# An encoder layer on one core: loads of the output projection issued two tiles ahead, stores moved to ScalarE's queue, and the down-projection's weight factors handed out in other places

## The chip, the cores and the metric

The kernel runs on one core of one Trainium2 chip. The metric is the device time of one execution in microseconds (us); below, times before are three runs and one profiled execution. The engines are TensorE (PE, with its weight loads as PEld), VectorE (DVE), ScalarE (ACT), GpSimd (POOL) and SyncE (SP), which here only issues DMAs. ACT and POOL can issue DMAs too; each engine works through its own list of instructions in order, and a DMA that waits holds up what is behind it on the engine that issues it.

## The reference

One layer of a hybrid encoder, for 2048 tokens of width 1024 and 16 meta tokens in front, all in float32:

```python
xn = rms_norm(h, g_pre_mix)
proj = xn @ w_in                       # q latent | kv latent | rotary key | S5 input
attn = mla_bidirectional(...)          # 8 heads, 512 columns
ssm  = S5 forward + backward, GELU, GLU   # 512 columns
mix = concat([rms_norm(attn, g1), rms_norm(ssm, g2)])
h = h + rms_norm(mix @ w_out, g_post_mix)
m = rms_norm(h, g_pre_mlp) @ w_mlp_up            # 1024 x 4096
m = square(relu(m)) @ w_mlp_down                 # 4096 x 1024
h = h + rms_norm(m, g_post_mlp)                  # meta tokens are dropped
```

## The kernel before, in words

Every float32 product is made of three matmuls: each operand is split (`split`, L125 to L127) into a rounded half, `h = copy(x)` on ACT (L126), and the rest, `l = x - h` on DVE (L127), and PE adds `h.h + h.l + l.h`. So each tile that goes into a product costs one ACT cast and one DVE subtraction; names end in `h` and `l` accordingly (`ah`, `al`, `wh`, `wl`).

The stages follow one another, with their edges overlapping: projections (to about 280 us of the span), attention with the S5 in its background (to about 1583), the output projection (to about 1850), the up-projection (to about 2508) and the down-projection (to the end). The function that emits a stage writes instructions in some order, but the kernel is built with `TileContext(nc, schedule_with_timeline_sim=True)`: a scheduler simulates the program and puts each engine's instructions in an order of its own, by the times at which they become ready there. So the order of the code sets which buffers there are and which loads exist, and the scheduler decides what stands where in each engine's list.

**Output projection.** There are 16 tiles of 128 tokens (`NT`). `out_tile(t)` (L1191) makes tile `t`, and prepares the attention half of tile `t+1` (`a_ops`, L1120) and the S5 half of tile `t+2` (`s_ops`, L1114). `s_ops` loads `sr` (128x4x128) from the DRAM buffer `SD`; `a_ops` loads `ar` from `AD` (attention's outputs, not divided by the sum yet) and, in two DMAs, `rb` from `RD2` (the reciprocals of the sums, broadcast over 64 rows each) and multiplies them on DVE (L1129). `halves` (L1104) splits the result, squares it on ACT (L1110) and sums it on DVE (`sq`, `aq`, L1111), for the norms of the two halves. `sr` and `rb` have one buffer each (`bufs=1`), `ar` two. PE makes `op` (L1183); ACT scales the attention half (`ot`, L1212) and DVE adds the S5 half (`o`, L1213). Then come the post norm (a square with a sum on ACT, `jk`, L1217; the root on POOL, L132 and L133; a product on DVE, L1219), the residual `xt`, whose load is emitted at the start of the tile (L1197) into one buffer, the store of `o` to `HD` (L1221, SP), and the pre norm of the MLP (`jk`, L1226; `hn`, L1228). `hn_T` (L1231) transposes `hn` on PE, ACT copies it to `hb`, and SP stores that to `HTD` in two DMAs (L1245). The first two tiles' S5 products are made ahead (`W["ps", t]`).

Attention's last work runs beside the first tiles: `X` (L612 to L614) adds up values from `ph` and `pl` (`pl = s - ph`, DVE L628); `o` is stored to `AD` and its sums to `RD` (L644, L645, SP), the sums come back as `rr` (L648, issued on POOL), DVE takes the reciprocal (L649) and POOL's queue writes `RD2` (L650).

**Up-projection.** 32 pairs, each with 84 matmuls for 256 hidden columns of 1024 tokens, in a scheme of seven products for 2x2 blocks (`pA`, `pB`, `pE`, `pF` are PSUM banks). `relu2` (L1352) takes a block through relu and square on ACT, makes sums on DVE and POOL (L1367 to L1373), and stores seven blocks of 256 KB per pair to `MD` (`put`, L1359, on SP). SP also loads 1 MB of weights (`raw`, L1254) and of transposed activations (`traw`, L1275).

**Down-projection.** 8 chunks `b` of 512 hidden columns, each with 4 groups `g` of 84 matmuls, again seven products (`pX`, `pY`, `pE`, `pF`, L1644) that are added to `acc`. `w_factors(b)` (L1531) is a generator: it loads the chunk's weights in two DMAs of 1 MB (`raw`) and yields 14 times, once for each weight factor (seven products times two halves `fp`). Four of the seven factors are sums of blocks: POOL makes them (`wst`, L1555), 14 instructions per chunk, then ACT and DVE split them. `m_factors` (L1565) loads `mraw` from `MD` and splits it. The loop over the groups passes `step` to `down`, which calls it after each product; there the generators are advanced:

```python
if g == 2 and i > 2:
    next(nwf, None)
elif g == 3:
    next(nwf, None)
    next(nwf, None)
```

Of the kernel before, what the change touches and what calls it, by code (L numbers as in the profile page):

```python
# [51 lines left out]
def hymba_layer_kernel(  # L52
# [1041 lines left out]
    def out_open():  # L1094
        ip = W["ip"] = ph.enter_context(pool("iO", 2, "right"))
        W["ep"] = ph.enter_context(pool("eO", 2, "right"))
        e1 = W["e1"] = ph.enter_context(pool("e1", 1, "right"))
        gpo = W["gpo"] = mk(e1, [128, D], "gpo")
        Y.dma_start(out=gpo, in_=g_post_mix[0].partition_broadcast(128))
        for t in range(2):  # L1100
            W["s", t] = s_ops(t)
            yield

    def halves(src, nm):  # L1104
# [6 lines left out]
        V.reduce_sum(out=sq, in_=src.rearrange("p k c -> p c k"), axis=AX.X)  # L1111
        return h, l, sq

    def s_ops(t):  # L1114
        cs = slice(t * 128, (t + 1) * 128)
        sr = W["ip"].tile([128, 4, 128], F32, tag="sr", name="sr", bufs=1)
        Y.dma_start(out=sr, in_=SD[:, cs].rearrange("(k p) c -> p k c", p=128))
        return halves(sr, "s")

    def a_ops(t):  # L1120
        cs = slice(t * 128, (t + 1) * 128)
        ar = W["ip"].tile([128, 4, 128], F32, tag="ar", name="ar")
        Y.dma_start(out=ar, in_=AD[:, cs].rearrange("(k p) c -> p k c", p=128))
        rb = W["ip"].tile([128, 4, 128], F32, tag="rb", name="rb", bufs=1)
        for b in range(2):
            src = RD2[b:b + 1, cs]
            Y.dma_start(out=rb[64 * b:64 * b + 64],
                        in_=bass.AP(src.tensor, src.offset, [[0, 64], [2 * 2048, 4], [1, 128]]))
        V.tensor_tensor(out=ar, in0=ar, in1=rb, op=ALU.mult)  # L1129
        return halves(ar, "a")  # L1130

# [57 lines left out]
        return sq, [out_mm(h, l, 4, half) for half in range(2)]  # L1189

    def out_tile(t, between):  # L1191
        if t + 1 < NT:
            W["a", t + 1] = a_ops(t + 1)
        if t + 2 < NT:
            W["s", t + 2] = s_ops(t + 2)
        xt = W["e1"].tile([128, D], F32, tag="xt", name="xt")
        Y.dma_start(out=xt, in_=xv[t // 8, t % 8])  # L1197
        sqs, ps = W.pop(("ps", t), None) or out_s(t)
        h, l, sqa = W.pop(("a", t))
        p = pa("ss")  # L1200
        T.matmul(out=p[:, 0:2], lhsT=sqa, rhs=ones)
        T.matmul(out=p[:, 2:4], lhsT=sqs, rhs=ones)
        s2 = sm.tile([128, 4], F32, tag="s2c", name="s2c")
        S.copy(out=s2, in_=p[:, 0:4])
        ra = rstd_of(s2[:, 0:1], 512)
        rb = rstd_of(s2[:, 2:3], 512, eps=4 * EPS)
        o = W["ep"].tile([128, D], F32, tag="o", name="o")
        for half in range(2):
            hs = slice(half * 512, (half + 1) * 512)
            p = out_mm(h, l, 0, half)  # L1210
            tm = W["e1"].tile([128, 512], F32, tag="ot", name="ot")
            S.activation(out=tm, in_=p, func=AF.Copy, scale=ra)  # L1212
            V.scalar_tensor_tensor(out=o[:, hs], in0=ps[half], scalar=rb, in1=tm, op0=ALU.mult, op1=ALU.add)  # L1213
        between()
        jk = W["e1"].tile([128, 512], F32, tag="ot", name="jk").bitcast(BF16)
        ss = sm.tile([128, 1], F32, tag="ss", name="ss")
        S.activation(out=jk, in_=o, func=AF.Square, accum_out=ss)  # L1217
        r = rstd_of(ss, D)
        V.scalar_tensor_tensor(out=o, in0=o, scalar=r, in1=W["gpo"], op0=ALU.mult, op1=ALU.mult)  # L1219
        V.tensor_tensor(out=o, in0=o, in1=xt, op=ALU.add)  # L1220
        Y.dma_start(out=HD[t], in_=o)  # L1221

        hn = wraw.tile([128, 8, 256], F32, tag="raw", name="raw")[:, 0:4].rearrange("p k c -> p (k c)") if t == NT - 1 else \
            W["e1"].tile([128, D], F32, tag="hn", name="hn", bufs=2)
        ss = sm.tile([128, 1], F32, tag="ss", name="ss")
        S.activation(out=jk, in_=o, func=AF.Square, accum_out=ss)  # L1226
        r = rstd_of(ss, D)
        V.scalar_tensor_tensor(out=hn, in0=o, scalar=r, in1=gpr, op0=ALU.mult, op1=ALU.mult)  # L1228
        return hn

    def hn_T(t, hn):  # L1231

        ct, i = t // 8, t % 8
        cs = slice((i % 4) * 128, (i % 4) * 128 + 128)
        ps = []
        for a in range(2):
            p = pa("hT")
            for k in range(4):
                T.transpose(out=p[:, k * 128:(k + 1) * 128], in_=hn[:, (4 * a + k) * 128:(4 * a + k + 1) * 128],
                            identity=ident)  # L1240
            ps.append(p)
        b = hn if t == NT - 1 else mk(tq, [128, D], "hb")
        for a in range(2):
            S.copy(out=b[:, a * 512:(a + 1) * 512], in_=ps[a])
            Y.dma_start(out=HTD[ct].rearrange("k p b c -> p k b c")[:, :, 2 * a + i // 4, cs],  # L1245
                        in_=b[:, a * 512:(a + 1) * 512].rearrange("p (k c) -> p k c", k=4))

    NP = FF // 256
# [24 lines left out]
    def s_load(ct, k):  # L1273
        RAW[ct, k] = raw = tst.tile([128, 4, 512], F32, tag="traw", name="traw")
        Y.dma_start(out=raw, in_=HTD[ct, k])  # L1275

    W["a", 0] = a_ops(0)
    for t in range(2):
        W["ps", t] = out_s(t)
# [72 lines left out]
    def relu2(c, src, n, odd, half):  # L1352

        S.activation(out=c, in_=src, func=AF.Relu)
        S.activation(out=c, in_=c, func=AF.Square)
        md = MD[n // NP, n % NP]

        def put(i, x):
            Y.dma_start(out=md[:, i], in_=x)  # L1359

        if (odd, half) != (0, 1):
            put({(0, 0): 0, (1, 0): 1, (1, 1): 5}[odd, half], c)
        blocks[odd, half] = c
        if len(blocks) == 4:
            a11, a12, a21, a22 = (blocks.pop(x) for x in ((0, 0), (1, 0), (0, 1), (1, 1)))
            s1, s2, s4 = rt(), rt(), rt()
            V.tensor_tensor(out=s1, in0=a21, in1=a22, op=ALU.add)  # L1367
            put(3, s1)
            V.tensor_tensor(out=a21, in0=a11, in1=a21, op=ALU.subtract)
            put(4, a21)  # L1370
            G.tensor_tensor(out=s2, in0=s1, in1=a11, op=ALU.subtract)
            put(2, s2)
            G.tensor_tensor(out=s4, in0=a12, in1=s2, op=ALU.subtract)  # L1373
            put(6, s4)
# [156 lines left out]
    def w_factors(b):  # L1531
# [9 lines left out]
        for first, *more in ((b11,), (b21,), (b22, (sub, b12), (add, b11)), (b12, (sub, b11)), (b22, (sub, b12)),  # L1541
                             (b22, (sub, b12), (add, b11), (sub, b21)), (b22,)):
            both = []
            for fp in range(2):
                def blk(x):
                    return raws[fp][:, x[0], x[1]]
# [5 lines left out]
                if more:  # L1552
                    st = wst.tile([128, 512], F32, tag="st", name="wst")
                    for op, x in more:
                        G.tensor_tensor(out=st, in0=src, in1=blk(x), op=op)  # L1555
                        src = st
                split(src, h, l)
                both.append((h, l))
# [134 lines left out]
    for n, (b, g) in enumerate(parts):  # L1693
# [4 lines left out]
        def step(i, behind):  # L1698
            if behind:
                next(nm, None)  # L1700
                if g == 2 and i > 2:
                    next(nwf, None)
                elif g == 3:
                    next(nwf, None)
                    next(nwf, None)
            elif n == 0:
                while len(WF) <= i:
# [1 line left out]

        down(b, g, step)  # L1710
        if g == 3:
            for _ in nwf:
                pass
            del WF[:7]


# [28 lines left out]
```

## Time and profile before

| | before |
|---|---|
| median of three runs | 3232.68 us (3231.8, 3232.68, 3236.42) |
| profiled execution | 3229.18 us |
| its span | 3227.4 us, so 1.8 us lie around it |
| mean granted TensorE clock | 0.964 |
| DMA | 329.93 MB, mean 102 GB/s |
| `MD` stores, `mraw` loads | 224 each, 256 KB |
| `HD` stores, `HTD` stores | 16 of 512 KB, 32 |
| weight loads of the down-projection | 16 of 1024 KB |

The profile shows one execution. In its tables an instruction stands as line, engine, operation, then output `<-` inputs; a wait is put down to the instruction or DMA that came last, in the form `[idle before <-releaser]`. "SPq" rows are DMAs that SP issued, with the time that issuing took, waits included. The table of windows gives, for each stretch of the span, the busy time of each engine with its count of instructions. The chain of waits goes back from the last instruction to what released it. Lines of all these are shown in the prediction where they are used.

### The profile page before, as it was taken

What the parts mean: (1) busy time and instruction counts of PE and PEld (TensorE: products, weight loads), DVE (VectorE), ACT (ScalarE), POOL (GpSimd) and SP (SyncE); (2) the same over time, 40 slices, a digit from 0 to 9 for tenths busy, and PEclk for the clock granted to TensorE, in tenths of its full rate; (3) what the DMA queues carried; (4) which work ended last, traced back from release to release, by engine and by line L of the source; (5) the groups of instructions that cost most, each with busy time, mean ns of one, the idle gap of its engine ahead of it and who ended that gap; (6) DMA issues with size and microseconds to landing.
All of it is one profiled execution on the core that took longest, in us unless ns stands there. A gap on an engine that the chain in (4) does not pass through costs nothing. (4 is left out here: it accounts for less than half of the span.)

```text
span 3227.4 us, 43434 instructions
## 1 busy us (share of the span) xinstructions
PE 2976.6 (92%) x14095; PEld 2361.9 (73%) x14095; DVE 2246.5 (70%) x3243; ACT 1763.7 (55%) x3345; POOL 1751.5 (54%) x2659
## 2 busy tenths in 40 slices
PE   6999988989999999999889789998999899999996
PEld 5899956656777766688667668887888677777774
DVE  6333278767888876675356587668767688888888
ACT  4333356988777799964445444545544433333343
POOL 4122245875888877600022287767767445555566
PEclk8999989999999999999999899999999999999998
DMA  4232231211000023231346445444544433333336
GB/s 151 62 86 74 69 78 27 60 43 33 24 15 26 26 70 90 67 117 49 70 146 191 148 129 174 154 152 149 173 150 151 133 114 111 117 112 111 111 121 202
DMA packets 300453, 329.93 MB, mean 102 GB/s; under 512 B 38736, under 2 KB 240848, under 8 KB 299200
## 3 DMA queue, kind: packets, MB, share of 16 engines
q1 hardware_dynamic: 298176, 325.44, 33.4%
q8 instruction: 111, 1.82, 0.2%
q10 hardware_dynamic: 1792, 1.57, 0.2%
q14 instruction: 118, 0.97, 0.1%
q0 software_dynamic: 256, 0.14, 0.0%
HBM read 206.47 MB, written 120.52 MB: 101 GB/s over the span
## 5 line engine op out<-in xcount | busy, mean ns | idle before, releaser
L628 DVE TENSOR_TENSOR pl<-s,ph 128x512 fp32r<-128x512 f32 x512 | 349.9, 685 | 164.8 <-ACT s L627 161.7
L624 ACT ACTIVATE ph<-s 128x512 fp32r<-128x512 f32 (+1 forms) x544 | 323.3, 595 | 168.7 <-PE s L622 155.5
L575 DVE TENSOR_REDUCE mx<-mxp 128x1 f32<-128x512 f32 x512 | 342.4, 683 | 55.7 <-PE mxp L574 52.6
L627 ACT ACTIVATE s<-s 128x512 f32<-128x512 f32 x512 | 304.1, 594 | 0.7
L126 ACT CAST ah<-mraw 128x512 fp32r<-128x512 f32 x224 | 138.8, 620 | 302.4 <-DMA mraw<-MD 216.0
L127 DVE TENSOR_TENSOR al<-mraw,ah 128x512 fp32r<-128x512 f32 x224 | 214.8, 964 | 73.5 <-ACT ah L126 68.2
L1266 POOL TENSOR_TENSOR st<-raw 128x512 f32<-128x512 f32 x120 | 179.9, 1501 | 135.2 <-DVE al L127 128.5
L620 PE MATMUL s<-ql,kh 96*128 96x512 f32 (+1 forms) x544 | 225.2, 414 | 14.7 <-ACT ZS L938 4.9
L612 PE MATMUL X<-pl,vt 128*65 128x512 f32 x512 | 209.4, 409 | 30.0 <-DVE pl L628 29.5
L621 PE MATMUL s<-qh,kl 96*128 96x512 f32 (+1 forms) x544 | 217.2, 399 | 0.0
L622 PE MATMUL s<-qh,kh 97*128 97x512 f32 (+1 forms) x544 | 214.5, 400 | 0.7 <-DMA qh<-nm 0.7
L574 PE MATMUL mxp<-kh,qh 96*128 96x512 f32 x512 | 199.0, 410 | 13.2 <-DVE mx L575 5.5
L132 POOL TENSOR_SCALAR rs_v<-ss 128x1 f32<-128x1 f32 (+1 forms) x98 | 21.8, 223 | 347.2 <-ACT kvn L325 119.1
L1666 POOL TENSOR_TENSOR acc<-acc,x 128x512 f32<-128x512 f32 x64 | 101.5, 1588 | 200.2 <-ACT x L1665 200.2
L613 PE MATMUL X<-ph,vt 128*64 128x512 f32 x512 | 204.8, 400 | 0.0
L1644 PE MATMUL pX<-wh,ah 128*128 128x512 f32 x384 | 160.2, 418 | 48.4 <-DVE acc L1653 48.1
L614 PE MATMUL X<-ph,vt 128*65 128x512 f32 x512 | 204.2, 399 | 0.0
L127 DVE TENSOR_TENSOR al<-st,ah 128x512 fp32r<-128x512 f32 x120 | 128.3, 1070 | 58.0 <-ACT ah L126 57.5
L1644 PE MATMUL pX<-wl,ah 128*128 128x512 f32 x384 | 156.7, 408 | 0.5 <-DVE wl L127 0.4
L126 ACT CAST ah<-st 128x512 fp32r<-128x512 f32 x120 | 74.1, 618 | 150.9 <-POOL st L1266 70.8
L1644 PE MATMUL pX<-wh,al 128*128 128x512 f32 x384 | 156.2, 407 | 0.0
L620 PEld LDWEIGHTS s<-ql,kh 96*128 96x128 f32 (+1 forms) x544 | 102.8, 189 | 62.2 <-DVE mx L575 7.5
(967 smaller groups left out, 9569.6 us busy)
## 6 DMA issues: line engine op xcount, KB each, us to landing
MD<-r SPq DMA_DIRECT2D x224, 256.0 KB
mraw<-MD SPq DMA_DIRECT2D x224, 256.0 KB
raw<-in_w_mlp_up_dram SPq DMA_DIRECT2D x32, 1024.0 KB
xt<-in_x_dram SPq DMA_DIRECT2D x32, 512.0 KB
raw<-in_w_mlp_down_dram SPq DMA_DIRECT2D x16, 1024.0 KB
ug<-UD SPq DMA_DIRECT2D x32, 256.0 KB
HD<-o SPq DMA_DIRECT2D x16, 512.0 KB
traw<-HTD SPq DMA_DIRECT2D x8, 1024.0 KB
```

The source lines that it names most:

```text
L126: S.copy(out=h, in_=src)
L127: eng.tensor_tensor(out=l, in0=src, in1=f(h), op=ALU.subtract)
L575: V.reduce_max(out=mxs[n][:, j, b:b + 1], in_=p, axis=AX.X)
L612: T.matmul(out=X[:65], lhsT=v[:, t, 0:65], rhs=pl_, start=(t == 0), stop=False)
L613: T.matmul(out=X[:64], lhsT=v[:, t, 65:129], rhs=ph_, start=False, stop=False)
L620: T.matmul(out=s[:m], lhsT=kh[0:96, cs], rhs=ql, start=True, stop=False)
L621: T.matmul(out=s[:m], lhsT=kl[:, cs], rhs=qh[0:96], start=False, stop=False)
L622: T.matmul(out=s[:m], lhsT=kh[:, cs], rhs=qh, start=False, stop=True)
L624: S.activation(out=ph_[:m], in_=s[:m], func=AF.Exp, scale=SCALE)
L627: S.activation(out=s, in_=s, func=AF.Exp, scale=SCALE)
L628: V.tensor_tensor(out=pl_, in0=s, in1=f(ph_), op=ALU.subtract)
L1644: T.matmul(out=ps, lhsT=x[:, c], rhs=y, start=(first and fp == 0 and j == 0), stop=(fp == 1 and j == 2), skip_group_check=not first)
```

## The change

Three parts.

1. Output projection. A new function `loads(t)` issues all of a tile's loads (`sr`, `xt`, `ar`, `rb`), and `out_tile(t)` calls it for `t+1` and `t+2` before it does anything else; `s_ops` and `a_ops` keep the arithmetic alone. `sr`, `rb` and `xt` have two buffers each now. The S5 half is prepared one tile ahead instead of two.
2. Stores. `HD`, `HTD` and three of the seven `MD` stores of a pair are issued by ACT (`S.dma_start`) and not by SP (`Y.dma_start`).
3. Down-projection. The generator of weight factors is advanced once per step, from the third step of group 2 over group 3 to the fourth of the next chunk's group 0, and not drained at the chunk's end. For chunk 0, the sums of `fp == 0` are made on DVE (V), not on POOL (G).

```diff
+    def sd_load(t):
+        cs = slice(t * 128, (t + 1) * 128)
+        W["sr", t] = sr = W["ip"].tile([128, 4, 128], F32, tag="sr", name="sr")
+        Y.dma_start(out=sr, in_=SD[:, cs].rearrange("(k p) c -> p k c", p=128))
+
     def s_ops(t):
-        cs = slice(t * 128, (t + 1) * 128)
-        sr = W["ip"].tile([128, 4, 128], F32, tag="sr", name="sr", bufs=1)
-        Y.dma_start(out=sr, in_=SD[:, cs].rearrange("(k p) c -> p k c", p=128))
-        return halves(sr, "s")
-
-    def a_ops(t):
+        return halves(W.pop(("sr", t)), "s")
+
+    def loads(t):
+
+        if ("x", t) in W:
+            return
+        if ("sr", t) not in W and t > 1:
+            sd_load(t)
+        W["x", t] = xt = tq.tile([128, D], F32, tag="xt", name="xt", bufs=2)
+        Y.dma_start(out=xt, in_=xv[t // 8, t % 8])
         cs = slice(t * 128, (t + 1) * 128)
         ar = W["ip"].tile([128, 4, 128], F32, tag="ar", name="ar")
         Y.dma_start(out=ar, in_=AD[:, cs].rearrange("(k p) c -> p k c", p=128))
-        rb = W["ip"].tile([128, 4, 128], F32, tag="rb", name="rb", bufs=1)
+        rb = W["ip"].tile([128, 4, 128], F32, tag="rb", name="rb")
+        W["ar", t] = ar, rb
         for b in range(2):
...
+    def a_ops(t):
+        ar, rb = W.pop(("ar", t))
         V.tensor_tensor(out=ar, in0=ar, in1=rb, op=ALU.mult)
...
     def out_tile(t, between):
+        for u in range(t + 1, t + 3):
+            if u < NT:
+                loads(u)
         if t + 1 < NT:
             W["a", t + 1] = a_ops(t + 1)
-        if t + 2 < NT:
-            W["s", t + 2] = s_ops(t + 2)
-        xt = W["e1"].tile([128, D], F32, tag="xt", name="xt")
-        Y.dma_start(out=xt, in_=xv[t // 8, t % 8])
+            if ("ps", t + 1) not in W:
+                W["s", t + 1] = s_ops(t + 1)
+        xt = W.pop(("x", t))
...
-        Y.dma_start(out=HD[t], in_=o)
...
         S.activation(out=jk, in_=o, func=AF.Square, accum_out=ss)
+        S.dma_start(out=HD[t], in_=o)
...
-            Y.dma_start(out=HTD[ct].rearrange("k p b c -> p k b c")[:, :, 2 * a + i // 4, cs],
+            S.dma_start(out=HTD[ct].rearrange("k p b c -> p k b c")[:, :, 2 * a + i // 4, cs],
...
-        def put(i, x):
-            Y.dma_start(out=md[:, i], in_=x)
+        def put(i, x, q=Y):
+            q.dma_start(out=md[:, i], in_=x)
 
         if (odd, half) != (0, 1):
-            put({(0, 0): 0, (1, 0): 1, (1, 1): 5}[odd, half], c)
+            put({(0, 0): 0, (1, 0): 1, (1, 1): 5}[odd, half], c, S)
...
-                        G.tensor_tensor(out=st, in0=src, in1=blk(x), op=op)
+                        (V if b == 0 and fp == 0 else G).tensor_tensor(out=st, in0=src, in1=blk(x), op=op)
...
-                if g == 2 and i > 2:
-                    next(nwf, None)
-                elif g == 3:
-                    next(nwf, None)
+                if (g == 2 and i > 2) or (g == 3 and i > 0) or (g == 0 and n > 0 and i < 4):
                     next(nwf, None)
...
         if g == 3:
-            for _ in nwf:
-                pass
             del WF[:7]
```

Since a scheduler decides the order, the places that matter are shown as the lists have them. First VectorE's list at the end of attention, from the first product `ar<-ar,rb` on (`pl` and `ph` are attention's, `ar`, `rb`, `al`, `aq` the attention half and `sr`, `sl`, `sq` the S5 half of an output tile; the numbers tell buffers apart). Before:

```order
L1129 TENSOR_TENSOR ar_19065<-ar_19065,rb_19067 128x512
L628 TENSOR_TENSOR pl_18954<-s_18948,ph_18952 128x512
L1111 TENSOR_REDUCE sq_18921<-sr_18915 128x128
L628 TENSOR_TENSOR pl_18966<-s_18960,ph_18964 128x512
L127 TENSOR_TENSOR al_19072<-ar_19065,ah_19071 128x512
L628 TENSOR_TENSOR pl_18978<-s_18972,ph_18976 128x512
L1111 TENSOR_REDUCE aq_19075<-ar_19065 128x128
L1129 TENSOR_TENSOR ar_19130<-ar_19130,rb_19132 128x512
L628 TENSOR_TENSOR pl_18990<-s_18984,ph_18988 128x512
L127 TENSOR_TENSOR sl_18939<-sr_18936,sh_18938 128x512
L127 TENSOR_TENSOR al_19137<-ar_19130,ah_19136 128x512
L628 TENSOR_TENSOR pl_19002<-s_18996,ph_19000 128x512
```

Now, from the same product on:

```order
L1143 TENSOR_TENSOR ar_19067<-ar_19067,rb_19069 128x512
L628 TENSOR_TENSOR pl_18954<-s_18948,ph_18952 128x512
L1112 TENSOR_REDUCE sq_18921<-sr_18915 128x128
L628 TENSOR_TENSOR pl_18966<-s_18960,ph_18964 128x512
L1112 TENSOR_REDUCE sq_18942<-sr_18936 128x128
L127 TENSOR_TENSOR al_19074<-ar_19067,ah_19073 128x512
L1143 TENSOR_TENSOR ar_19134<-ar_19134,rb_19136 128x512
L628 TENSOR_TENSOR pl_18978<-s_18972,ph_18976 128x512
L628 TENSOR_TENSOR pl_18990<-s_18984,ph_18988 128x512
L1112 TENSOR_REDUCE aq_19077<-ar_19067 128x128
L127 TENSOR_TENSOR al_19150<-ar_19134,ah_19149 128x512
L628 TENSOR_TENSOR pl_19002<-s_18996,ph_19000 128x512
```

The first product still stands ahead of the same `pl`. The second product stands one `pl` earlier, and no longer behind `aq` of the first. The next rows of the new list are `aq_19153` and then the third product; before, the third product came next, and the second's `aq` behind it. The line numbers of the new file are some 14 higher here.

Second, SyncE's list of DMAs, from the load of `rb` for the second product to the store of `RD`. Before:

```order
L1127 DMA rb_19132<-RD2_78 64x4x128 x2
L1117 DMA sr_18936<-SD_76 128x4x128
L1123 DMA ar_19218<-AD_75 128x4x128
L1127 DMA rb_19220<-RD2_78 64x4x128 x2
L1127 DMA rb_19308<-RD2_78 64x4x128
L1117 DMA sr_19143<-SD_76 128x4x128
L1127 DMA rb_19308<-RD2_78 64x4x128
L1123 DMA ar_19306<-AD_75 128x4x128
L1127 DMA rb_19437<-RD2_78 64x4x128 x2
L644 DMA AD_75<-o_19038 64x512
L645 DMA RD_77<-o_19038 1x512
```

Now:

```order
L1138 DMA rb_19136<-RD2_78 64x4x128 x2
L1138 DMA rb_19145<-RD2_78 64x4x128 x2
L1118 DMA sr_19139<-SD_76 128x4x128
L1118 DMA sr_19220<-SD_76 128x4x128
L1138 DMA rb_19226<-RD2_78 64x4x128 x2
L1133 DMA ar_19143<-AD_75 128x4x128
L1133 DMA ar_19224<-AD_75 128x4x128
L1138 DMA rb_19314<-RD2_78 64x4x128 x2
L1138 DMA rb_19443<-RD2_78 64x4x128 x2
L644 DMA AD_75<-o_19038 64x512
L645 DMA RD_77<-o_19038 1x512
```

What was one `rb` after the other, each behind a product, is now issued with two buffers ahead of the loads of `sr` and `ar`; the stores of `AD` and `RD`, which attention's end goes through, still stand behind the `rb` of two further tiles. The stores of `HD` and `HTD` further down are no longer in this list; they stand on ScalarE's, `HD` behind the second `jk`, `HTD` behind the copies to `hb`.

Third, GpSimd's list at chunk 0 of the down-projection, from the last sum of the up-projection (`r`) on; `wst` are the factor sums, `raw_26528` and `raw_26530` the weights of `fp` 0 and 1 of chunk 0, `raw_27160` and `raw_27162` those of chunk 1, `acc` the results. Before:

```order
L1373 TENSOR_TENSOR r_26658<-r_26629,r_26657 128x512
L1555 TENSOR_TENSOR wst_26788<-raw_26528 128x512
L1555 TENSOR_TENSOR wst_26794<-raw_26530 128x512
L1555 TENSOR_TENSOR wst_26822<-raw_26528 128x512
L1555 TENSOR_TENSOR wst_26828<-raw_26530 128x512
L1555 TENSOR_TENSOR wst_26858<-raw_26528 128x512
L1555 TENSOR_TENSOR wst_26858<-wst_26858,raw_26528 128x512
L1555 TENSOR_TENSOR wst_26866<-raw_26530 128x512
L1555 TENSOR_TENSOR wst_26858<-wst_26858,raw_26528 128x512
L1555 TENSOR_TENSOR wst_26866<-wst_26866,raw_26530 128x512
L1666 TENSOR_TENSOR acc_26685<-acc_26685,x3_26838 128x512
L1666 TENSOR_TENSOR acc_26685<-acc_26685,x3_26847 128x512
```

Now:

```order
L1390 TENSOR_TENSOR r_26658<-r_26629,r_26657 128x512
L1572 TENSOR_TENSOR wst_26794<-raw_26530 128x512
L1572 TENSOR_TENSOR wst_26828<-raw_26530 128x512
L1572 TENSOR_TENSOR wst_26866<-raw_26530 128x512
L1572 TENSOR_TENSOR wst_26866<-wst_26866,raw_26530 128x512 x2
L1683 TENSOR_TENSOR acc_26685<-acc_26685,x3_26838 128x512
L1683 TENSOR_TENSOR acc_26685<-acc_26685,x3_26847 128x512
L1572 TENSOR_TENSOR wst_27292<-raw_27160 128x512
```

The sums of `raw_26528` are gone from this list and stand on VectorE's, and the first sums of chunk 1 have moved ahead of the next `acc`. From the end of chunk 0 on, each engine's list of the changed kernel holds the same instructions in the same order as before.

More of the change, by code (lines that the diff above doesn't have):

```diff
@@ L1112, in halves @@
         return h, l, sq
+    def sd_load(t):
+        cs = slice(t * 128, (t + 1) * 128)
+        W["sr", t] = sr = W["ip"].tile([128, 4, 128], F32, tag="sr", name="sr")
+        Y.dma_start(out=sr, in_=SD[:, cs].rearrange("(k p) c -> p k c", p=128))
     def s_ops(t):
-        cs = slice(t * 128, (t + 1) * 128)
-        sr = W["ip"].tile([128, 4, 128], F32, tag="sr", name="sr", bufs=1)
-        Y.dma_start(out=sr, in_=SD[:, cs].rearrange("(k p) c -> p k c", p=128))
-        return halves(sr, "s")
-    def a_ops(t):
+        return halves(W.pop(("sr", t)), "s")
[3 more added lines that the diff above has]
+        if ("sr", t) not in W and t > 1:
+            sd_load(t)
+        W["x", t] = xt = tq.tile([128, D], F32, tag="xt", name="xt", bufs=2)
+        Y.dma_start(out=xt, in_=xv[t // 8, t % 8])
         cs = slice(t * 128, (t + 1) * 128)
@@ L1275, in s_load @@
         Y.dma_start(out=raw, in_=HTD[ct, k])
+    loads(0)
     W["a", 0] = a_ops(0)
```

## The prediction, made before the changed kernel had run

> **What bounds the kernel now.** The page first: TensorE (PE) is busy for 92% of the span.
>
> ```profile
> span 3227.4 us, 43434 instructions
> PE 2976.6 (92%) x14095; PEld 2361.9 (73%) x14095; DVE 2246.5 (70%) x3243; ACT 1763.7 (55%) x3345; POOL 1751.5 (54%) x2659
> ```
>
> The other 8%, 251 us, is what a change of order can win. The table of windows (length, then busy time of PE, PEld, DVE, ACT, POOL, then PE's clock, DMA share, GB/s) says where it lies; the rows are the end of attention, the output projection, the up-projection, chunk 0 of the down-projection with the start of chunk 1, and most of chunks 1 to 7.
>
> ```profile
> 1560.00:1640.00 80.00, 64.66 (x302) 50.12 (x301) 29.17 (x44) 27.37 (x53) 4.51 (x10) 0.91 0.39 92
> 1640.00:1860.00 220.00, 185.69 (x847) 148.39 (x846) 135.67 (x146) 105.94 (x201) 64.33 (x128) 0.94 0.58 166
> 1860.00:2500.00 640.00, 615.71 (x2663) 505.46 (x2664) 480.89 (x509) 315.95 (x553) 463.25 (x301) 0.98 0.47 154
> 2500.00:2640.00 140.00, 122.96 (x500) 97.57 (x499) 99.61 (x123) 62.69 (x112) 63.11 (x42) 0.93 0.41 127
> 2640.00:3150.00 510.00, 476.48 (x2036) 388.29 (x2035) 423.50 (x543) 177.27 (x315) 280.82 (x192) 0.97 0.38 114
> ```
>
> PE idles 15 us around attention's end, 34 in the output projection, 24 in the up-projection, 17 around chunk 0 and 34 in the chunks behind it. PE's timeline gives the pieces at attention's end (start, duration, instruction, idle before and its releaser):
>
> ```profile
> 1587.97 0.69 PE L612 MATMUL X<-pl,vt 128*65 128x512 f32 x1 [4.10 <-DVE pl L628]
> 1588.46 0.63 PE L613 MATMUL X<-ph,vt 128*64 128x512 f32 x1
> ...
> 1597.49 0.44 PE L612 MATMUL X<-pl,vt 128*65 128x512 f32 x1 [1.51 <-DVE pl L628]
> 1597.78 0.39 PE L613 MATMUL X<-ph,vt 128*64 128x512 f32 x1
> ...
> 1608.54 0.69 PE L612 MATMUL X<-pl,vt 128*65 128x512 f32 x1 [5.84 <-DVE pl L628]
> ...
> 1627.35 0.50 PE L1183 MATMUL op<-woh,ah 128*128 128x512 f32 x1 [2.60 <-ACT ot L1212]
> ...
> 1631.66 0.50 PE L1183 MATMUL op<-woh,sh 128*128 128x512 f32 x1 [1.28 <-DVE o L1213]
> ```
>
> The second matmul behind the gap of 4.10 us takes 0.63 us, the second behind that of 1.51 us 0.39. About ten matmuls go that slowly, 0.24 us more each, so a long gap costs some 2 us more than it shows. [...]
>
> VectorE (DVE) was late with `pl` because it stood at a product of the output projection that waits for a load:
>
> ```profile
> 1586.62 0.69 DVE L1129 TENSOR_TENSOR ar<-ar,rb 128x512 f32<-128x512 f32 x1 [7.59 <-DMA rb<-RD]
> ...
> 1596.14 0.69 DVE L1129 TENSOR_TENSOR ar<-ar,rb 128x512 f32<-128x512 f32 x1 [4.32 <-DMA rb<-RD]
> ...
> 1605.35 0.69 DVE L1129 TENSOR_TENSOR ar<-ar,rb 128x512 f32<-128x512 f32 x1 [5.44 <-DMA rb<-RD]
> ...
> 1615.62 0.69 DVE L1129 TENSOR_TENSOR ar<-ar,rb 128x512 f32<-128x512 f32 x1 [6.41 <-DMA ar<-AD]
> ...
> 1629.93 0.35 DVE L649 RECIPROCAL rr<-rr 128x32 f32<-128x32 f32 x1 [11.26 <-DMA rr<-RD]
> ```
>
> The four products come 9.2 to 10.3 us apart, since `rb` has one buffer: a load waits for the product before it, then takes 8.5 us. SyncE's (SP's) queue shows that, and that attention's last stores sit behind it:
>
> ```profile
> 1587.34 1.24 SPq L1127 DMA_DIRECT2D rb<-RD  x2
> ...
> 1596.86 9.78 SPq L1127 DMA_DIRECT2D rb<-RD  x3
> ...
> 1608.02 0.60 SPq L1123 DMA_DIRECT2D ar<-AD  x1
> 1616.33 1.23 SPq L1127 DMA_DIRECT2D rb<-RD  x2
> ...
> 1618.73 0.44 SPq L645 DMA_DIRECT2D RD<-o  x1
> ```
>
> **The start of the output projection.** The forecast is that the first wait stays: `ar(0)` still stands ahead of a `pl`, and its `rb` is still issued where it was. PE keeps the 4.10 us and the 2 us of slow clock. Then, with a second `rb` buffer: `rb(1)` is issued behind `rb(0)`, no longer behind the product at 1586.6, so product 1 can run at about 1590 instead of 1596.1. `rb(2)` follows product 0 at 1587.4 and takes 8.5 us (1587.34 to 1596.14 is 8.8, 1596.86 to 1605.35 is 8.5): product 2 at about 1596 to 1597 instead of 1605.4. For product 3 `ar(3)` waits for `aq(1)`, now ahead of product 2, so it is issued at about 1597 and takes what the row at 1608.02 took to the product at 1615.62, 7.6 us: about 1605 instead of 1615.6. Behind it SP issues the last `rb`, `AD`, `RD`, as before 3.1 us from product to `RD` (1615.62 to 1618.73): 1608 at most, and `RD` goes 11 us earlier than 1618.73. The reciprocal followed `RD` by 11.2 us (1629.93 less 1618.73), and behind it on DVE are the first `o` products that free PE's banks (1.28 us, at 1631.66).
>
> Check from PE's side: between 1583.9 and 1631.7 it has 47.8 us, less gaps of 15.3 (4.10, 1.51, 5.84, 2.60, 1.28) and 4 of slow clock, so 28.5 of matmuls. With only the first gap left that ends at 1583.9 + 4.1 + 2 + 28.5 = 1618.5, 13 us earlier than 1631.7, so DVE's chain at 11 is the later. I take -11.5, from -5 (loads slower together) to -13.
>
> **Tiles 1 to 3 and 8 to 10.** The largest gaps behind it:
>
> ```profile
> 1643.86 0.79 PE L1183 MATMUL op<-woh,ah 128*128 128x512 f32 x1 [3.20 <-ACT s2c L1204]
> ...
> 1654.18 0.50 PE L1183 MATMUL op<-woh,sh 128*128 128x512 f32 x1 [2.19 <-DVE o L1213]
> ...
> 1661.65 0.50 PE L1183 MATMUL op<-woh,ah 128*128 128x512 f32 x1 [1.21 <-ACT s2c L1204]
> ...
> 1667.36 0.96 PE L1239 MATMUL hT<-ident,hn 128*128 128x128 f32 x4 [2.68 <-ACT ot L1212]
> ...
> 1774.65 0.50 PE L1183 MATMUL op<-woh,ah 128*128 128x512 f32 x1 [2.65 <-ACT s2c L1204]
> ...
> 1778.87 1.22 PE L1239 MATMUL hT<-ident,hn 128*128 128x128 f32 x8 [1.21 <-DVE hn L1228]
> ...
> 1840.44 1.94 PE L1239 MATMUL hT<-ident,hn 128*128 128x128 f32 x8 [7.93 <-DVE hn L1228]
> ```
>
> The first four are 9.3 us and end on the sums `s2c` and on `o`, which need both loads of a tile. Loads two tiles ahead take the load away but not the chain POOL, ACT, DVE: -5.5, from 0 to -9.3. The two at 1774 to 1779, 3.9 us, follow the first two 1 MB `traw` loads on SP: -3, from 0 to -3.9. Tiles between have 0.5 us each on `o`; for DVE's moved product I take -1 in all, from 0 to -3. The 7.93 at the last tile is the norm chain with no next tile to cover it, unchanged.
>
> **Stores on ScalarE (ACT).** Three of seven `MD` stores of each of 32 pairs, 16 `HD` and 32 `HTD`: 144 issues. One such issue on ACT's queue is in the trace, and a steady stretch of the up-projection:
>
> ```profile
> L443 ACTq DMA_DIRECT2D QD<-qo x16: 310/310/362, 398.4 to 435.7; - x16
> ```
> ```profile
> 1960.00:1980.00 20.00, 20.00 (x90) 16.57 (x89) 12.79 (x15) 10.60 (x19) 13.76 (x10) 1.00 0.50 169
> ```
>
> At 0.31 us, 96 in the up-projection are 30 us of ACT time, 1 us per pair of 20 us in which ACT works 10.6 and PE 20.00: hidden by PE, 0, with -2 (SP's loads no longer behind stores) to +8 as bounds (30 us times the 24 in 640 of the stage in which PE does wait is 1.1; a store that waits for its own result or for a completion slot could be several times that). The casts `ah` and the relus queue behind the issue; DVE and PE wait for them, and if ACT were full each issue would cost its 0.31. In the output projection 3 issues a tile, 1 us, fall in a 13 us tile with ACT half busy: +1; behind the last tile the two `HTD` stand ahead of the first casts of the up-projection: +0.7. [...]
>
> **Down-projection.** Gaps of chunk 0, then the chain's pieces at one chunk boundary and the waits of 2640 to 3150:
>
> ```profile
> 2513.99 1.22 PE L1644 MATMUL pY<-wh,ah 128*128 128x512 f32 x2 [5.67 <-ACT wh L126]
> ...
> 2534.32 1.10 PE L1644 MATMUL pF<-wh,ah 128*128 128x512 f32 x2 [3.95 <-ACT wh L126]
> ```
> ```profile
> 2681.09 4.72 POOL wst L1555 x3
> ...
> 2697.57 7.02 DMA raw<-in_w_mlp_down_dram
> ```
> ```profile
> PE pX L1644 <- DVE acc L1653: 33.1, 12, 5.2
> ```
>
> Six boundaries lie in that window; at them spreading the factors would pay: `step` now hands out one factor per product, from the third product of group 2 to the fourth of the next chunk, where it handed out two. But the scheduler sorts instructions by its own simulated times, and from the end of chunk 0 on each engine's list reads the same before and after. With the same lists, the 1 MB load that ACT waits for and the 33.1 us on `acc` stay: 0. What does move is chunk 0: half of its `wst` sums, 7 of 14, go from POOL to DVE. The rows are POOL's sums and, of the waits of 2500 to 2640, what they cost ACT's casts.
>
> ```profile
> L1555 POOL TENSOR_TENSOR wst<-raw x64: 1285/1299/1759, 2482.7 to 3105.3; 128x512 f32<-128x512 f32 x64
> ```
> ```profile
> ACT wh L126 <- POOL wst L1555: 16.3, 9, 5.1
> ```
>
> At 1.30 us seven fewer are 9 us of POOL; at the 0.69 of DVE's product of the same shape (1586.62) seven more are 5 of DVE, beside casts that now wait for POOL 16.3 us in all. The gap of 3.95 goes by this with its 2 us of slow clock; that of 5.67 stays, since its cast stands behind the last relu in ACT's list before and after; DVE's own 5 us take 1 back. I take -5, from 0 (DVE is the later then) to -12 (both gaps and their slow clock).
>
> **The sum.** -11.5 - 5.5 - 3 - 1 + 1 + 0.7 + 0 + 0 - 5 = -24.3 us. The profiled run took 3229.2 us (its span and 1.8 around it) and would take 3204.9; the median of the runs, 3232.7, lies 3.5 above it, so 3208 us is the forecast for a median.
>
> **Rivals.**
> - Late start (0.17). The loads of two tiles issued together share bandwidth, `rb` stays near 8.5 us apart, and the reciprocal goes only 5 us earlier. Then -5 - 2 + 1 + 0.7 - 3 is -8: 3224. For it: product 0 still waits. Against it: 92 GB/s in that window.
> - Nothing measurable (0.10). As above, and DVE takes back in chunk 0 what POOL gains: within 0.2% (6.5 us, about what a measurement of this kernel can tell from none), 3230.
> - The spread works after all (0.03): the 33.1 us on `acc` go, and with them at most the slow clock of that window, 0.03 of 510 or 15 us: -24 - 33 is 3175, and 3160 with the clock. Against it the identical lists.
> - Slower (0.07). [...]
>
> The forecast itself has 0.63. **Range:** 3188 (all terms near their good ends, -24.3 less 20) to 3226 (the late start's end); outside lie the spread, the loss and nearly all of the no-change case, 0.2. Faster by over 0.2%: 0.63 + 0.17 + 0.03 = 0.83; within: 0.10; slower: 0.07.
>
> **What would show it.** Right: products `ar<-ar,rb` about 1587, 1590, 1597, 1605; the reciprocal near 1619; the gap of 5.84 gone and that of 4.10 still there; up-projection pairs at 20.00 busy; the boundary gaps on `acc` unchanged, near 33 us. Wrong: the reciprocal later than 1625, up-projection windows under 20.00, or shorter chunks from chunk 1 on.

## The result, and the profile after

| | before | changed |
|---|---|---|
| median | 3232.93 us (four runs, 3231.8 to 3236.42) | 3213.05 us (four runs, 3209.27 to 3214.77) |
| ratio, 95% interval | 1 | 0.9935 (0.9918 to 0.9952) |
| profiled execution, its span | 3229.18, 3227.4 us | 3214.64, 3212.9 us |

By these medians the change makes the kernel 20 us faster; 24 had been forecast. The profiled pair differs by only 14.5 us: the one before lies 3.7 us below its median, the one after 1.6 above. Against the larger groups of runs of the kernel before that were made for the experiments (medians 3228.13 to 3231.19 us) the gain would be 15 to 18 us.

Where the time went is read by stages from TensorE's timelines: from the start of the last score matmul of attention (`s`, L622) to the first matmul of the up-projection (`c`), from there to its last one, then chunk 0 (up to the 337th matmul of the down-projection, since a chunk has 4 groups of 84) and the rest. The third row is experiment `e5_spread`, whose lists are the same as before.

| us | output projection | up-projection | chunk 0 | chunks 1 to 7 |
|---|---|---|---|---|
| before | 266.0 | 658.4 | 91.3 | 610.0 |
| changed | 253.5 | 659.6 | 88.5 | 606.8 |
| `e5_spread` | 267.4 | 660.0 | 91.3 | 603.6 |

Two executions of one list differ by 1.4 us in the first stage and by 6.4 in the last, so only the 12.5 us of the output projection are clear in this pair; that the 2.8 us of chunk 0 are real as well, the other profiles show (`e3_sums`). Inside it, the positions of the tiles (the matmul that sums `sq`, counted from the same score matmul) tell more: tile 4 comes at 70.1 us in place of 92.5, tile 11 at 173.2 in place of 185.3. So 22 us are won by tile 4, and 10 are lost again between tiles 4 and 11, which now take 14.7 us each and took 13.3.

First the start. VectorE's timeline of the changed kernel, the four products and the reciprocal (line numbers are those of the new file, some 14 higher):

```profile
1588.21 0.69 DVE L1143 TENSOR_TENSOR ar<-ar,rb 128x512 f32<-128x512 f32 x1 [6.04 <-DMA rb<-RD]
...
1592.54 0.69 DVE L1143 TENSOR_TENSOR ar<-ar,rb 128x512 f32<-128x512 f32 x1
...
1604.51 0.69 DVE L1143 TENSOR_TENSOR ar<-ar,rb 128x512 f32<-128x512 f32 x1 [6.77 <-DMA ar<-AD]
1605.12 0.68 DVE L628 TENSOR_TENSOR pl<-s,ph 128x512 fp32r<-128x512 f32 x1
1605.72 0.68 DVE L1143 TENSOR_TENSOR ar<-ar,rb 128x512 f32<-128x512 f32 x1
...
1620.18 0.35 DVE L649 RECIPROCAL rr<-rr 128x32 f32<-128x32 f32 x1 [5.12 <-DMA rr<-RD]
```

The serial round of `rb` is gone: the second product waits for nothing. The third now waits for `ar`, which SP issued just ahead of the fourth's, and the last `pl` behind it makes TensorE wait. Attention's end then waits for that: ScalarE copies `o` from `X` when TensorE has it, and SP's store of it, with `RD` behind, waits for the copy (SP's list, TensorE's, ScalarE's, and SP's waits from 1580 to 1612: us in total, times, longest):

```profile
1595.40 2.73 SPq L1133 DMA_DIRECT2D ar<-AD  x2
1605.23 2.64 SPq L1138 DMA_DIRECT2D rb<-RD  x4
...
1611.82 0.44 SPq L645 DMA_DIRECT2D RD<-o  x1
```
```profile
1589.56 0.69 PE L612 MATMUL X<-pl,vt 128*65 128x512 f32 x1 [3.49 <-DVE pl L628]
...
1605.86 0.66 PE L612 MATMUL X<-pl,vt 128*65 128x512 f32 x1 [3.12 <-DVE pl L628]
```
```profile
1610.68 0.58 ACT L642 COPY o<-X 65x512 f32<-65x512 f32 x1 [2.18 <-PE X L609]
```
```profile
SPq L644 <- ACT o L642: 3.4, 1, 3.4
```

The two gaps of 3.49 and 3.12 us are TensorE's only ones there, 6.6 us in place of 15.3; behind both its matmuls took 0.63 us and not 0.39, for 6.0 and for 3.4 us, as for 4.3 us behind the 4.10 us before. In this execution attention ended 2.2 us later than in the one before, so the reciprocal, 9.75 us earlier by the clock, is 11.9 earlier from attention's end.

Then the steady tiles. A tile of the changed kernel in VectorE's timeline, then SP's DMAs for that product and TensorE's gap:

```profile
1677.04 0.74 DVE L1229 SCALAR_TENSOR_TENSOR o<-op,rs_r,ot 128x512 f32<-128x512 f32 x1
1680.26 0.69 DVE L1143 TENSOR_TENSOR ar<-ar,rb 128x512 f32<-128x512 f32 x1 [2.47 <-DMA ar<-AD]
1680.87 1.04 DVE L1112 TENSOR_REDUCE sq<-sr 128x128 f32<-128x512 f32 x1
1681.83 0.74 DVE L1229 SCALAR_TENSOR_TENSOR o<-op,rs_r,ot 128x512 f32<-128x512 f32 x1
```
```profile
1672.73 0.35 SPq L1130 DMA_DIRECT2D xt<-in_x_dram  x1
1673.73 0.36 SPq L1133 DMA_DIRECT2D ar<-AD  x1
```
```profile
1682.62 0.50 PE L1197 MATMUL op<-woh,sh 128*128 128x512 f32 x1 [1.04 <-DVE o L1229]
```

The product stands between the two `o` products of a tile and waits 2.47 us there. The second `o` is late, and with it the bank that TensorE needs. Before, the same product stood ahead of `hn`, and TensorE lost 0.2 us on `o`:

```profile
1690.99 0.69 DVE L1129 TENSOR_TENSOR ar<-ar,rb 128x512 f32<-128x512 f32 x1 [1.91 <-DMA ar<-AD]
1691.60 0.68 DVE L127 TENSOR_TENSOR sl<-sr,sh 128x512 fp32r<-128x512 f32 x1
1692.20 1.27 DVE L1228 SCALAR_TENSOR_TENSOR hn<-o,rs_r,gpr 128x1024 f32<-128x1024 f32 x1
```
```profile
1695.17 0.66 PE L1239 MATMUL hT<-ident,hn 128*128 128x128 f32 x4 [0.21 <-DVE o L1213]
```

In windows of 20 us (PE, PEld, DVE, ACT, POOL, clock, DMA share, GB/s) the same shows as less work of TensorE, before and changed:

```profile
1700.00:1720.00 20.00, 19.37 (x93) 15.77 (x92) 13.27 (x16) 9.56 (x19) 7.35 (x14) 1.00 0.81 210
```
```profile
1700.00:1720.00 20.00, 18.18 (x81) 13.85 (x81) 12.95 (x15) 9.43 (x19) 6.05 (x14) 1.00 0.52 152
```

The up-projection is as before, TensorE full beside the ScalarE stores, and so are the waits on `acc` in 2640 to 3150, 33.6 us after 33.1:

```profile
1960.00:1980.00 20.00, 20.00 (x90) 16.53 (x90) 14.97 (x15) 10.14 (x18) 12.56 (x9) 1.00 0.50 163
```
```profile
PE pX L1661 <- DVE acc L1670: 33.6, 13, 5.3
```

### The profile page after: what moved, and what is told of

Read it like the earlier page. It is cut to its first block, busy times and chain, and to the rows that moved or that the text cites. A ratio compares the mean times of both kernels' runs of the same rounds, so it can differ in the third digit from the quotient of the medians.

```text
span 3212.9 us, 43329 instructions
## 1 busy us (share of the span) xinstructions
PE 2982.4 (93%) x14095; PEld 2366.1 (74%) x14095; DVE 2250.1 (70%) x3250; ACT 1765.9 (55%) x3345; POOL 1742.4 (54%) x2652
## 5 line engine op out<-in xcount | busy, mean ns | idle before, releaser
L622 PE MATMUL s<-qh,kh 97*128 97x512 f32 (+1 forms) x544 | 215.6, 402 | 0.7 <-DMA qh<-nm 0.7
```

The lines of the kernel that those rows point to most:

```text
L622: T.matmul(out=s[:m], lhsT=kh[:, cs], rhs=qh, start=False, stop=True)
```

## The experiments

Theory A: the loss between tiles 4 and 11 comes from the place of the product, which the moved stores changed. Theory B: it comes from the early loads. Ratios are to runs of the kernel before on the same chip, whose medians were 3228.13, 3231.19 and 3229.47 us for the three groups below.

| | median us | ratio (95%) | output projection | tile 4 at | each, 4 to 11 |
|---|---|---|---|---|---|
| before | 3232.93 | 1 | 266.0 | 92.5 | 13.3 |
| changed | 3213.05 | 0.9935 (0.9918 to 0.9952) | 253.5 | 70.1 | 14.7 |
| `e1_loads` | 3216.25 | 0.9968 (0.9956 to 0.9980) | 251.9 | 80.0 | 13.2 |
| `e2_stores` | 3238.22 | 1.0034 (1.0021 to 1.0047) | 274.6 | 88.8 | 14.4 |
| `e3_sums` | 3225.27 | 0.9991 (0.9983 to 1.0000) | 266.1 | 92.3 | 13.2 |
| `e4_md_only` | 3215.01 | 0.9963 (0.9951 to 0.9975) | 255.3 | 81.7 | 13.4 |
| `e5_spread` | 3227.36 | 0.9995 (0.9986 to 1.0004) | 267.4 | 94.0 | 13.1 |
| `e7_am1` | 3185.36 | 0.9863 (0.9848 to 0.9878) | 226.8 | 67.9 | 12.3 |
| `e8_mulG` | 3222.11 | 0.9980 (0.9970 to 0.9990) | 267.0 | 75.1 | 15.4 |
| `e9_ar3sr1` | 3212.68 | 0.9952 (0.9940 to 0.9965) | 255.2 | 80.5 | 14.3 |
| `e10_before_am1` | 3210.23 | 0.9947 (0.9934 to 0.9961) | 248.8 | 75.7 | 13.1 |
| `e11_loads_am1` | 3202.35 | 0.9918 (0.9904 to 0.9932) | 239.3 | 67.5 | 13.1 |
| `e12_hd_sp` | 3219.11 | 0.9969 (0.9956 to 0.9981) | 258.4 | 73.3 | 14.6 |

What tells the tiles of 14.3 us and more from those of 13.4 and less is VectorE's list (`e8_mulG`, without the product in that list, aside). For one tile (`o2` its two products, `l`, `q` the rest `al` and the sum `aq` of an attention half, `h2` its `hn`, `A` the product `ar` by `rb`, each with its tile's number) it reads:

```
before       o2 o2 l5 q5 A7 h2
e1_loads     o2 o2 l5 q5 A7 h2
e2_stores    o2 A6 o2 l5 q5 h2
changed      o2 A6 o2 l5 q5 h2
e12_hd_sp    o2 A6 o2 l5 q5 h2
e9_ar3sr1    o2 A7 o2 l5 q5 h2
e7_am1       o2 o2 l5 q5 A6 h2
```

**One part at a time.** `e1_loads` takes the first part of the diff alone.

> Only the loads of the output projection are changed (part 1); stores and the down-projection are as before. Theory A: the changed kernel gains 19 us by the fourth tile and gives 9 back between tiles 3 and 10 because the moved stores made the scheduler place the product ar<-ar,rb between the two o products. Here that product stands ahead of hn as before, so the 19 us stay: about 3214 us, 13.3 us from tile to tile. Theory B: the 9 us are given back because the early loads of xt and the second buffers crowd the load of ar, whatever the stores do: tiles 14.7 us apart and about 3223 us.

`e2_stores` takes the second alone, on the kernel before:

```diff
-        Y.dma_start(out=HD[t], in_=o)
...
+        S.dma_start(out=HD[t], in_=o)
...
-            Y.dma_start(out=HTD[ct]...
+            S.dma_start(out=HTD[ct]...
...
+            put({(0, 0): 0, (1, 0): 1, (1, 1): 5}[odd, half], c, S)
```

> Only the stores HD, HTD and three of seven MD are moved to ScalarE (part 2). Theory A: the product ar<-ar,rb now stands between the two o products without any gain at the start: tiles 14.7 us apart from the third or fourth on, some 9 to 15 us slower than before, 3242 to 3248 us. Theory B: no change, 3233 us, tiles 13.3 us apart.

The tiles came out as theory A says, and B is out: 13.2 us with the loads alone, 14.4 with the stores alone. The stores alone make the kernel slower by 0.34%. From 1640 to 1780, the waits of the kernel before on the load and on `o`, then those of `e2_stores` on the same:

```profile
DVE ar L1129 <- DMA ar<-AD: 30.1, 10, 6.9
PE hT L1239 <- DVE o L1213: 3.7, 7, 0.7
PE op L1183 <- DVE o L1213: 2.2, 1, 2.2
```
```profile
DVE ar L1129 <- DMA ar<-AD: 21.4, 9, 5.8
...
PE op L1183 <- DVE o L1213: 9.3, 5, 4.4
```

VectorE waits longer for the load in the kernel before, 30.1 us against 21.4 in `e2_stores`, and yet TensorE loses less on `o` there, 5.9 us in all against 10.2 (0.9 of them at `hT`, not shown). So the length of the wait alone does not tell what it costs.

But the sum that theory A gave for `e1_loads` was wrong: tile 4 comes at 80.0 us there, not at 70.1. A good half of the gain up to tile 4 is the loads' (12.5 of 22.4), and 10 us of it need the stores as well. The next run says so again.

`e4_md_only` is the changed kernel with `HD` and `HTD` on SP:

> The changed kernel with HD and HTD back on SyncE (MD stays on ScalarE). Theory A: the product ar<-ar,rb stands ahead of hn again and the 9 us are not given back: about 3204 us. Theory B: 3213 us, as the changed kernel, tiles 14.7 us apart.

13.4 us per tile, as A has it, but tile 4 at 81.7, so nothing is won on the changed kernel. In the output projection the moved stores give with one hand, up to tile 4, and take with the other.

`e3_sums` changes one line of the kernel before:

```diff
-                        G.tensor_tensor(out=st, in0=src, in1=blk(x), op=op)
+                        (V if b == 0 and fp == 0 else G).tensor_tensor(out=st, in0=src, in1=blk(x), op=op)
```

> Only the seven factor sums of chunk 0 are moved from GpSimd to VectorE. If they are what chunk 0 gained in the changed kernel: 3 us less, about 3230 us, all of it between 2500 and 2640 us. If the 3 us came from the loads of mraw that stand closer together: within 1 us of before, 3233 us.

The ratio leaves 0 to 0.17%, and chunk 0 takes 89.8 us after 91.3 in both executions of the lists of before. The other profiles agree: the six kernels with these sums on GpSimd (before, `e1_loads`, `e2_stores`, `e5_spread`, `e10_before_am1`, `e11_loads_am1`) have 91.2 to 92.6 us in chunk 0, the seven with them on VectorE 87.1 to 89.8. So the sums are worth about 3 us, 1.5 of them seen in `e3_sums` itself. Why it isn't more can be read from the changed kernel's waits from 2487 to 2627: the casts waited 16.3 us for POOL's sums before, and now wait 9.0 for POOL's and 8.3 for VectorE's, and both gaps of TensorE stay, a little shorter (5.67 and 3.95 before).

```profile
ACT wh L126 <- POOL wst L1572: 9.0, 8, 2.7
ACT wh L126 <- DVE wst L1572: 8.3, 3, 4.6
...
PE pY L1661 <- ACT wh L126: 5.3, 1, 5.3
...
PE pF L1661 <- ACT wh L126: 3.7, 1, 3.7
```

`e5_spread` is the third part without the sums:

```diff
-                if g == 2 and i > 2:
-                    next(nwf, None)
-                elif g == 3:
-                    next(nwf, None)
+                if (g == 2 and i > 2) or (g == 3 and i > 0) or (g == 0 and n > 0 and i < 4):
                     next(nwf, None)
```

> Only the places where the weight factors are handed out are changed (part 3 without the sums on VectorE). Each engine's list is the same as before, from the first instruction to the last. Theory: no change, within 0.1% of before; its profile is then a second sample of the kernel before and shows how far stages differ between two executions of the same lists. Rival (the spread works in some way that the lists do not show): 30 us or more faster, and chunks of the down-projection shorter than 85 us.

No change, as the lists say.

**Why the product waits.** Theory C: its load is late because `ar`'s buffer comes free late, so a third buffer is the cure. Theory D: the scheduler moves the product up to where its own clock has the load landed, so more buffers move both. Both runs have one buffer for `sr`, to make room: with two, a third `ar` leaves 14.5 KB per partition for a pool of 16 (`e6_ar3`).

`e9_ar3sr1`:

```diff
-        ar = W["ip"].tile([128, 4, 128], F32, tag="ar", name="ar")
+        ar = W["ip"].tile([128, 4, 128], F32, tag="ar", name="ar", bufs=3)
```

> The changed kernel with a third buffer for ar and one for sr. Theory C (the load of ar is late because its buffer comes free late): the product no longer waits, tiles 3 to 11 take 12.3 to 13.3 us, time near the run with the product in a tile of its own (ratio to before about 0.987). Theory D (the scheduler hoists the product to where its own clock has the load landed): VectorE's list has A of four tiles ahead between the two o products, so the wait stays, tiles 14 us or more, ratio to before about 0.993 as the changed kernel.

`e7_am1`:

```diff
-        V.tensor_tensor(out=ar, in0=ar, in1=rb, op=ALU.mult)
-        return halves(ar, "a")
+        am = W["ip"].tile([128, 4, 128], F32, tag="am", name="am", bufs=1)
+        V.tensor_tensor(out=am, in0=ar, in1=rb, op=ALU.mult)
+        return halves(am, "a")
```

> The changed kernel with the product of ar and rb written to a tile of its own with one buffer (and one buffer for sr, to make room). It can't be placed ahead of the sum aq of the tile before, and ar comes free at the product, so its load is issued about a tile earlier. Theory D: VectorE waits for no load any more between the two o products, tiles 3 to 11 take 12.5 to 13 us in place of 14.7, and the time is 15 us or more below the changed kernel. Rival (the load is late by the bandwidth that xt and the HD store take): the wait stays, tiles 14 us or more, time within 4 us of the changed kernel.

With three buffers the list has `A7` where it had `A6`, the product still waits between the two `o`, and nothing is won. The load for it is still issued right behind an `aq`, 6.2 us ahead of the product, since the third buffer went to a product one tile further ahead (VectorE's timeline with that `aq`, then SP's):

```profile
1678.13 1.09 DVE L1112 TENSOR_REDUCE aq<-ar 128x128 f32<-128x512 f32 x1
...
1682.55 0.74 DVE L1229 SCALAR_TENSOR_TENSOR o<-op,rs_r,ot 128x512 f32<-128x512 f32 x1
1685.47 0.69 DVE L1143 TENSOR_TENSOR ar<-ar,rb 128x512 f32<-128x512 f32 x1 [2.17 <-DMA ar<-AD]
1686.08 1.07 DVE L1112 TENSOR_REDUCE sq<-sr 128x128 f32<-128x512 f32 x1
1687.06 0.74 DVE L1229 SCALAR_TENSOR_TENSOR o<-op,rs_r,ot 128x512 f32<-128x512 f32 x1
```
```profile
1679.24 0.36 SPq L1133 DMA_DIRECT2D ar<-AD  x1
```

With a tile of its own the product can't go ahead of `aq`, which frees that tile, while `ar` is freed by the product itself. SP's queue and VectorE's timeline of `e7_am1`: the load issued at 1662.68 follows the product that freed its buffer (1661.96), and with two buffers the load for the product at 1674.29 is the one of 1650.62, 24 us earlier. The product waits for no load, and TensorE is at 20.00 of 20:

```profile
1650.62 0.36 SPq L1133 DMA_DIRECT2D ar<-AD  x1
...
1662.68 0.36 SPq L1133 DMA_DIRECT2D ar<-AD  x1
```
```profile
1674.29 0.69 DVE L1144 TENSOR_TENSOR am<-ar,rb 128x512 f32<-128x512 f32 x1
1676.11 1.28 DVE L1245 SCALAR_TENSOR_TENSOR hn<-o,rs_r,gpr 128x1024 f32<-128x1024 f32 x1 [1.13 <-POOL rs_r L133]
1677.31 0.68 DVE L127 TENSOR_TENSOR sl<-sr,sh 128x512 fp32r<-128x512 f32 x1
1677.91 0.74 DVE L1230 SCALAR_TENSOR_TENSOR o<-op,rs_r,ot 128x512 f32<-128x512 f32 x1
1678.70 1.08 DVE L1112 TENSOR_REDUCE sq<-sr 128x128 f32<-128x512 f32 x1
1679.69 0.74 DVE L1230 SCALAR_TENSOR_TENSOR o<-op,rs_r,ot 128x512 f32<-128x512 f32 x1
```
```profile
1700.00:1720.00 20.00, 20.00 (x100) 16.74 (x99) 16.22 (x19) 12.35 (x23) 5.96 (x12) 1.00 0.60 170
```

This version beats both kernels: 1.37% faster than before, and over its tiles of 12.3 us TensorE hardly idles: from 1660 to 1740 it is busy for 80.00 us of 80, in the changed kernel for 72.8. Theory C is out: a third buffer is no cure. The lists are as theory D has them; that the scheduler goes by the landing on its own clock fits them, but no run shows it by itself. The new tile does two things at once, it holds the product back and frees `ar` earlier, and what each is worth was not tried apart.

`e8_mulG` puts the product on GpSimd (`G.tensor_tensor` in place of `V.tensor_tensor`):

> The changed kernel with the product of ar and rb on GpSimd in place of VectorE. Theory D: VectorE no longer waits for the load, so o is not held up by it; but GpSimd's own list has the two roots of every tile behind the product, and a product costs it about 1.3 us and the wait. The gap on o of 1.0 us per tile goes, gaps on s2c and hn may grow: between 12 us faster than the changed kernel and 5 us slower. Rival as for the run before: within 4 us of it, the wait for ar showing on GpSimd and o still late.

It came out worse than expected, only 0.2% faster than before. The wait moved to GpSimd's list, where the roots stand behind it, and `o` waits for those. The profile gives no releaser for GpSimd's wait; that it is the load is likely, since nothing else about the product was changed. GpSimd's row and VectorE's answer to it:

```profile
1685.60 1.29 POOL L1143 TENSOR_TENSOR ar<-ar,rb 128x512 f32<-128x512 f32 x1 [5.03 <-issue]
```
```profile
1687.84 1.28 DVE L1235 SCALAR_TENSOR_TENSOR o<-o,rs_r,gpo 128x1024 f32<-128x1024 f32 x1 [3.97 <-POOL rs_r L133]
```

**What the other parts are worth once the product is out of the way.** `e10_before_am1` is the kernel before with the edit of `e7_am1` (its `sr` has one buffer already), `e11_loads_am1` is `e1_loads` with that edit.

> The kernel before, and only the product of ar and rb written to a tile of its own with one buffer; rb still has one buffer, stores on SyncE. If the place of the product is what costs in the tiles, they take 12.3 us in place of 13.3 and the early ones less than 18: 12 to 20 us faster than before (ratio 0.994 to 0.996), with the start (one rb after the other) still late. If the loads ahead or ScalarE's stores are needed for that too: within 5 us of before.

> The loads of the output projection alone (part 1, stores on SyncE, down-projection as before), with the product in a tile of its own and one buffer for sr. If the moved stores are worth something by themselves, this is slower than the changed kernel with the same edit (ratio to before 0.986) by over 5 us; if all they did was to move the product in the lists, it is equal to it within 3 us, tiles 12.3 us.

Three lines on the kernel before give 0.53%, nearly as much as the whole change. The time was as expected, but the tiles were not: from tile 4 to 11 they take 13.1 us and not 12.3, and the gain lies ahead of tile 4, which comes at 75.7 us in place of 92.5. The loads ahead add 0.29% to that. From there to `e7_am1`, which has the moved stores (and the sums and the spread, worth about 0.1% by the runs above), it is another 0.55%: tiles 13.1 to 12.3 us, and 80.4 to 72.9 us from tile 11 to the end. So the stores on ScalarE are worth something beyond the product's place, against what I had put second in that expectation. By what they gain it is not settled: they leave SP's list and they change the scheduler's order in other places as well.

`e12_hd_sp` is the changed kernel with `HD` alone back on SP, and lists of TensorE and VectorE that keep the product's place:

> The changed kernel with only the HD stores back on SyncE. VectorE's list has the product in the same places, TensorE's is the same from first to last. If the 14.7 us per tile come from the order, they stay and the time is that of the changed kernel (ratio to before about 0.993). If they come from ScalarE's issuing of 512 KB stores beside the xt and ar loads, tiles go to 13.3 us and the time falls by 9 us.

The tiles stay at 14.6 us, so it is the order and not the queue of `HD` that makes them long. Nor is it `HTD` on ScalarE, which `e7_am1` has too, with tiles of 12.3 us. But the run is slower than the changed kernel, 6 us by the medians and 0.34% by the ratios, which I had not expected: in the two profiles tile 4 comes 3 us later, and tile 12 follows tile 11 after 20.8 us in place of 17.6. (Up to tile 4 it seems to be `HTD` that matters most: 81.7 us with both stores on SP in `e4_md_only`, 73.3 with `HTD` on ScalarE here.) Why `HD` on SP costs there is not settled; that the loads behind it in SP's list come later is likely, and only argued.

## Why the prediction was right, and where it wasn't

- **The start (-11.5) and tiles 1 to 3 (-5.5).** Right in kind, together -17 and measured -22.4 up to tile 4, but split otherwise. Tile 2's first matmul, where the sum for the start ended (1631.66), came 9.2 us earlier, counted from the last score matmul. From there to tile 4 it was 13.2 us, more than the 9.3 given as the most: TensorE's gaps between these two points went from 9.8 us to 0.3, and the slow matmuls behind them, for which that term held nothing, went too (seven of 0.60 to 0.79 us behind the gap of 3.20, three of 0.53 to 0.78 behind those of 2.68 and 0.56; now none is over 0.50). "Loads two tiles ahead take the load away but not the chain POOL, ACT, DVE" was the step that failed there.
- **Product 2.** The reciprocal came 11.9 us earlier from attention's end; 11 were forecast. That these agree is partly luck. The step that named the wait of product 2 failed: not `rb` but `ar` came last, at 1604.5 in place of 1597, since `ar(2)` is issued behind the `aq` that frees its buffer too. So the gap of 5.84 became 3.12 and did not go, and with it `X` and attention's last `o` came later. `RD` was not set by product 3, which came right behind (1605.72 against 1605 forecast), but by that `o`: it was issued 6.1 us behind the product and not 3.1, and 9.1 us earlier from attention's end, not 11. The way from `RD` to the reciprocal then took 8.4 us where 11.2 had been taken over from the kernel before; why, the runs leave open. The first gap stayed, 3.49 for 4.10.
- **Steady tiles (-1) and tiles 8 to 10 (-3).** Wrong in sign: +10 us. The failed step is "for DVE's moved product I take -1". I saw it leave the way from `o` to `hn` and did not ask what it had moved in front of: the second `o` of the tile. `e2_stores` shows that place without the loads (14.4 us a tile), `e1_loads` the loads without that place (13.2).
- **Stores on ScalarE.** 0 in the up-projection was right: 20.00 of 20, and 659.6 us for 658.4. ScalarE's 96 issues of `MD` took 0.33 us each by the median, about 31 us in all, and 1.24 at the longest. That a store there waits for a completion slot, as the bound of +8 allowed for, no run shows. In the output projection +1 was wrong both ways. Issue time was not the matter there (by the medians 0.35 us for an `HD` on ScalarE, 0.33 on SP): the stores changed the scheduler's order, which cost, and once the product's place was mended the kernel with them was 0.55% faster than the one without, about 0.1% of that being the sums.
- **Chunk 0 (-5).** About half of it: 2.8 us in the pair. I took the gap of 3.95 us to go with POOL's sum; 3.7 of it stayed, since 8.3 us of the casts' waits went to VectorE's sums.
- **Chunks 1 to 7 (0).** Right, and for the reason given: `e5_spread` has the same lists and the same time. The 3.2 us between the two profiles say nothing of the change, since `e5_spread` differs from before by 6.4.
- **The sum.** -24.3 forecast, -20 by the medians, -14.5 in the profiled pair; the range held both. By the pair, the errors were -5 up to tile 4, +12 in the rest of the output projection and +2 in chunk 0; +1 and -3 in the two stages put at nothing are within what two executions of one list differ by, and attention ended 2.2 us later. That the total comes near the forecast is luck in part, since errors of both signs made it up. What lies between 14.5 and 20 can't be given to a stage: runs of the kernel before scatter from 3222 to 3236 us on one chip.

## What to carry to other kernels

When a scheduler orders an engine's list, read after each edit what a waiting instruction has been put in front of; here one product of 0.69 us that waits for its load cost about 11 us, 0.3%, between tiles 4 and 11 by its place (14.7 us a tile with it, 13.2 in `e1_loads`). A third buffer for its input did not help against that, since the product moved up by a tile as well; an output tile that comes free only at the right time did hold it back. Undo each part of a change by itself even when the whole is a gain: here the stores alone were a loss, and a gain only after three other lines.

## What the runs showed of the hardware

An `ar` load of 256 KB took 3.0 us from issue to product when SP issued it ahead of `xt` (1687.98 to 1690.99, before) and 6.5 us when 512 KB of `xt` had been issued 1 us ahead of it and an `HD` store of 512 KB beside it (1673.73 to 1680.26, changed). That the one slows the other was not tried by itself. I had reckoned with 7.6 us at attention's end and with nothing in the steady tiles.

Two executions of the same lists took 610.0 and 603.6 us for chunks 1 to 7 of the down-projection, 1.0% of that stage; a difference of that size between two profiles says nothing about a change.
